# Eight copying transfers issued one stage earlier, and one weight load moved behind an exchange, in a two-layer decoder trunk

## The chip, the cores and the metric

The kernel runs on one core of one Trainium2 chip. The metric is the device time in microseconds of one execution. Before the change it is 1097.91 us as the median of three runs (1097.39 to 1098.72 us). One further execution was recorded by the hardware profiler; all rows in this document come from such recorded executions.

The engines are named as in the profile: PE is the matrix engine (PEld its weight loads), DVE the vector engine, ACT the scalar engine, POOL the GpSimd engine and SP the sync engine, which here only issues transfers.

## The reference

The input x is 512 tokens of 1024 float32 numbers. It passes two layers; each has an attention mixer and a gated feed-forward part:

```python
for i in range(DEPTH):                       # DEPTH = 2
    h = rms_norm(x, pre_g);  h = mixer_i(h);  x = x + rms_norm(h, post_g)
    h = conv_ffn(rms_norm(x, ffn_pre_g[i]), w_up, conv_w, conv_b, w_down)
    x = x + rms_norm(h, ffn_post_g[i])
```

Layer 0's mixer is latent attention beside differential attention. Layer 1's mixer is dilated attention in three groups of four heads beside stick-breaking attention with four heads. In the dilated part each group has its own softmax, and the groups are merged by weights made from all three groups' largest scores and denominators. The feed-forward part multiplies by w_up (1024 x 5632), runs a causal convolution of width 3 over the tokens, gates one half with the other, and multiplies by w_down (2816 x 1024).

## The kernel before

**Tiles.** The 512 tokens are four tiles of 128, taken in the order 3, 2, 1, 0 (ORDER, the names X[3] to X[0]). Every float32 product is made of three matrix products: a value is split into a rounded high part and the remainder, and mm3 (lines 325 to 327) issues high x high, high x low and low x high.

**Weights.** The class Weights feeds blocks of 128 x 1024. load issues one transfer on SP's queue (line 62) into a staging buffer wraw, of which there are three; split makes the parts from it, with a cast on ACT (line 84) and a subtraction on DVE (line 85), and only then is the staging buffer free. ahead says how many blocks are made beyond the one in use. W is the main list; W2, made in the second layer, holds the first two blocks of that layer's output projection and shares the staging buffers with W.

**The weight sums.** Sixteen of the 22 pairs of up-projection blocks of each layer are multiplied by a scheme with seven half-size products in place of eight, which needs sums of the quarters of w_up. The DMA engines make these sums in DRAM while the core computes: sum_steps lists eight steps (copy or accumulate) for each of six chunks of weights, and each step is one transfer of POOL's queue (line 164), of 768 KB for the first four chunks. In the list for a layer, the first step of all four chunks comes first, then the second step, and so on. Steps one and two are plain copies from the input into two different sums; step three accumulates onto the first copy. A small transfer of one number, the mark (line 173), can be put ahead: POOL's queue waits there until that number has been made, which holds back all that follow. Layer 1's first four chunks are ordered by make_sums(1, range(4), ...) in odd (line 1627): the mark, whose number comes from sv (the copy to lead, line 1626), and 32 transfers. Chunk 4 follows in odd behind a mark made of shares, and chunk 5 at the start of the second feed-forward part.

**The end of layer 0.** ffn(0) ends with the last four units of the down projection, tile by tile. The order is written out by hand for PE, DVE, ACT and POOL (the tail, from line 812 on). For each tile, part_of squares and sums on ACT and multiplies by the gain on DVE, and rstd (lines 238 to 241) makes one over the root on POOL. add_to (line 818) adds the normed result to X on DVE. Then mean_square of X (ACT, line 250, and POOL again), normed (DVE, line 822) and turned (PE transposes, line 273) make the transposed input of the next layer. r1 and r0 are the roots of tiles 1 and 0 of this norm, q1 the list of the two roots of the next layer's first norm for X[1] and X[0]. The last transposes stand between products of odd's first projection: tile_V for tiles 3, 2 and 1 calls what is in turns at its steps 4, 5 and 6. So POOL's order is r1, the root for X[1], r0, the root for X[0].

**The dilated part of layer 1.** Stick-breaking attention comes first, then the dilated groups (lines 1876 on), again in an order written by hand, SP included. Four projections cq and ck are made; score12 and softmax12 score groups 1 and 2, with the maxima and sums in st12. Those are laid out by residue of the token modulo 4, and group 0's statistics st0 by plain token tile, so the two are exchanged through DRAM: exchange(n, src) writes a small table (line 1802) and exchange_back(n, dst) reads it in the other layout (line 1805), both on SP's queue. share (lines 1786 to 1794) makes from both the weight of each group, scale0 (line 1820) and scale12 (line 1849) multiply the scores by it, and turn0 and turn12 transpose the scores on PE (lines 1830 and 1859). tile_V makes the values of groups 1 and 2 from four blocks of od_w_v12 and writes them re-ordered by transfers of SP (line 1899). In the third of the four projections stands W2.load(), which issues the load of the second block of W2. W2.next() behind the first share makes its parts (wo, from the same lines 84 and 85).

**Scheduling.** Where no order is written by hand, the framework's planner orders an engine's instructions by their dependencies and its own costs; SP's queue at the end of ffn(0) is such a case.

Of the kernel before, what the change touches and what calls it, by code (L numbers as in the profile page):

```python
# [98 lines left out]
def trunk(tc, A, out):  # L99
    nc = tc.nc  # L100
    PE, ACT, DVE, POOL = nc.tensor, nc.scalar, nc.vector, nc.gpsimd

    with ExitStack() as top:
# [28 lines left out]
        lead = cst.tile([P, 72], F32, tag="lead", name="lead")  # L132
# [13 lines left out]
        sums_of = {}  # L146

        def sum_steps(layer, chunks, mark=None, copies_first=False):

            wide = "(a q) c -> a (q c)"  # L150
            if layer not in sums_of:
                sums_of[layer] = [[dpool.tile([n * P, S], F32, tag=f"ws{layer}{j}{c}", name="ws")
                                   for c, n in enumerate(CHUNKS[layer])] for j in range(4)]
            tiles = sums_of[layer]

            def move(c, j, src, op):
                if src is None:
                    src = tiles[0][c][:]
                elif src < 0:
                    src = tiles[1][c][:]  # L160
                else:
                    at = sum(CHUNKS[layer][:c]) * P
                    src = A[f"ffn_up_q{layer}"][src, at:at + CHUNKS[layer][c] * P]
                nc.gpsimd.dma_start(tiles[j][c][:].rearrange(wide, q=4), src.rearrange(wide, q=4), accum_op=op,  # L164
                                    max_dma_last_dim=8192)

            steps = [(0, 3, ALU.bypass), (2, 2, ALU.bypass), (0, 2, ALU.add), (2, 0, ALU.add), (1, None, ALU.bypass),
                     (1, 0, ALU.add), (3, -1, ALU.bypass), (3, 1, ALU.add)]
            if copies_first:
                steps[4:] = [(1, 0, ALU.bypass), (3, 1, ALU.bypass), (1, None, ALU.add), (3, -1, ALU.add)]  # L170
            moves = [lambda c=c, step=step: move(c, *step) for step in steps for c in chunks]
            if mark is not None:
                moves.insert(0, lambda: nc.gpsimd.dma_start(tiles[0][chunks[0]][0:1, 0:1], mark))
            return moves

        def make_sums(layer, chunks, mark, left=0):
            moves = sum_steps(layer, chunks, mark)
            with tc.manual_schedule(engines={POOL.engine}):
                while len(moves) > left:
                    moves.pop(0)()  # L180
            return moves
# [20 lines left out]
                    up += [(A["ffn_w_up"][layer, f, z], 1024) for z in range(2)]  # L202
            return (up + [lambda n=n: down[layer](n) for n in range(4 * HF)])

        down, last_rstd = {}, {}
        units = []
        units += [(A["ev_w_c"][u], 832) for u in range(4)]
        units += [(A["ev_w_dqk"][0, 0], 1024), (A["ev_w_dqk"][0, 1], 1024)]
# [24 lines left out]
        def rstd(ms, more=None, r=None, eps_r=None, eps=epst):  # L233
            n = ms.shape[1]
            v = chp.tile([P, 4], F32, tag="rv", name="rv", bufs=4)
            if r is None:
                r = chp.tile([P, 4], F32, tag="rr", name="rr", bufs=4)
            POOL.tensor_tensor(v[:, :n], ms, eps[:, :n], ALU.add)  # L238
            if more is not None:
                POOL.tensor_tensor(v[:, :n], v[:, :n], more, ALU.add)  # L240
            POOL.tensor_tensor(r[:, :n], v[:, :n], mhalf[:, :n], ALU.pow)
            if eps_r is not None:
                POOL.tensor_tensor(eps_r, v[:, :n], epst[:, :n], ALU.mult)
            return r
# [147 lines left out]
        def ffn(layer, xnT, pending, final):  # L392
            with ExitStack() as es:
# [423 lines left out]
                def add_to(i, t, r):  # L817
                    DVE.scalar_tensor_tensor(X[i][:], t[:], r[:, 0:1], X[i][:], ALU.mult, ALU.add)

                def normed(i, r, t):  # L820
                    for c in (slice(0, S), slice(S, D)):
                        DVE.scalar_tensor_tensor(t[:, c], X[i][:, c], r[:, 0:1], g_next[:, c], ALU.mult, ALU.mult)
# [23 lines left out]
                c1 = bank_done("c", 1, between=turn(3, t3))  # L846
                part_of(t1, m1, 1, t1[:, S:], g_post, lambda: normed(2, q2, t2q))
                r1 = rstd(m1[:, 0:1], m1[:, 1:2])
                W.ahead(W.pos + 4)
                add_to(1, t1, r1)  # L850
                q1 = []

                def last():
                    part_of(t0, m0, 0, (uu[:, 1], c1), g_post, lambda: normed(1, q1[0], t1))
                    r0 = rstd(m0[:, 1:2], m0[:, 0:1])
                    add_to(0, t0, r0)


# [682 lines left out]
        def odd(xnT, pending, order):  # L1541
            xh, xl = xnT
            with ExitStack() as es:
# [44 lines left out]
                def proj_T(*args):  # L1588
                    for _ in T_parts(*args):
                        pass  # L1590
# [33 lines left out]
                DVE.tensor_copy(tri[:], trif[:])  # L1624

                ACT.copy(lead[0:1, 1:2], sv[0:1, 0, 0:1])
                make_sums(1, range(4), lead[0:1, 1:2])


                for u in range(2):  # L1630
# [173 lines left out]
                def exchange_back(n, dst):  # L1804
                    nc.sync.dma_start(dst[:].rearrange("p a b c -> p a (b c)"), views[n][1 - n])
# [68 lines left out]
                W2 = Weights(nc, None, [(A["od_w_out"][k], 1024) for k in range(2)], 2, wpool)  # L1874
# [5 lines left out]
                with tc.manual_schedule(engines={PE.engine, DVE.engine, ACT.engine, POOL.engine, nc.sync.engine}):  # L1880
                    for n, (x, t) in enumerate((x, t) for x in range(2) for t in (cq, ck)):
                        proj_T(t[x], (-0.125, 1.0)[t is ck], False, t is cq)
                        if n % 2 == 0:
                            softmaxes = score12(n // 2)
                        softmaxes.pop(0)()
                        if n == 1:
                            wo2.append(W2.next())
                        if n == 2:
                            W2.load()
                    exchange(1, st12)  # L1890
                    depth, W.depth = W.depth, 0
                    project = proj_V()

                    def tile_V(i, tag):
                        a = project(i, tag=tag)
                        st = chp.tile([P, 512], F32, tag="s", name="vst")
                        ACT.copy(st[:], a)
                        for r in range(4):
                            nc.sync.dma_start(cv12[32 * i:32 * i + 32, r], st[r::4, :])

                    tile_V(3, "a")
                    exchange_back(1, on)
                    for i, banks in zip((3, 2, 1, 0), ("ss", "tn", "aa", "oa")):
                        score0(i, banks)
                    exchange(0, st0)
                    tile_V(2, "s")
                    exchange_back(0, by_r)
                    W.load()
                    W.load()
                    share(st0, on, 0, slice(0, 4))  # L1910
                    for i in ORDER[:2]:
                        scale0(i)
                    wo2.append(W2.next())
                    tile_V(1, "s")
                    for i in ORDER[2:]:
                        scale0(i)
                    share(st12, by_r, 1, slice(0, 4))
                    tile_V(0, "a")

                    moves = sum_steps(1, (4,), shares[1][0:1, 0, 0:1], True)  # L1920
                    halves = [glob.tile([P, 2, 4, 256], F32, tag=tag, name="pt") for tag in ("xh", "xl")]
                    turned_to += [spare[:, 0], spare[:, 1]]
                    turned_to += [sb.tile([P, 4, 256], F32, tag=tag, name="pt")[:] for tag in ("sl", "sh")]
                    turned_to += [x[:, n] for x in halves for n in range(2)]
                    fours = [(hp, rp) for hp in range(2) for rp in range(2)]
                    pts = []
                    for n, i in enumerate(ORDER):
                        pts.append(turn0(i)())
                        scale12(*fours[n])
                        for _ in range((3, 1, 1, 1)[n]):  # L1930
                            moves.pop(0)()
                    for a in fours:
                        pts.append(turn12(*a)())
                    W.ahead(W.pos + 2)
                    oT = [bank("os"[k], "oT") for k in range(2)]
                    oG = [[ap.tile([P, S], F32R, tag=f"{t}{k}", name="og") for k in range(2)] for t in ("cq", "ck")]
                    for u in range(2):
                        for value, pt in zip([value0(i) for i in ORDER] + [value12(*a) for a in fours], pts):
                            value(pt, u)
                        split(oG[0][u][:], oG[1][u][:], oT[u])  # L1940
# [50 lines left out]
        xnT = ffn(0, *xnT, False)  # L1991
        xnT = odd(*xnT)
        ffn(1, *xnT, True)


# [99 lines left out]
```

## Time and profile before

| | |
|---|---|
| median of three runs | 1097.91 us |
| profiled execution | 1096.47 us |
| its span, first to last instruction | 1094.7 us |
| mean granted clock of PE | 0.998 |
| busy: PE, DVE, ACT, POOL | 1085.6, 907.5, 647.8, 129.1 us |
| transfers on POOL's queue | 67.1 MB |
| transfers on SP's queue | 147.7 MB |

The span is what instructions cover; the profiled execution has 1.8 us around it. A row of the timeline names start, duration, engine, line, operation, and "out<-in" by the program's tile names; what stands in brackets is the time the engine stood idle before it and what released it. A row of the waits names the waiting engine and line, what it waited for, the total, how often, and the longest. A row of the windows gives a stretch, its length, the busy time of PE, PEld, DVE, ACT and POOL, the granted clock, the share of the 16 DMA engines in use and GB/s. A row of transfers names what is moved, the queue, how many, KB each, and the median time from issue to landing.

### The profile page before, as it was taken

To read this page: it belongs to the slowest core of one execution; us is meant where nothing else is said; L and a number is where in the kernel's file an instruction comes from. 1 tells how busy PE (TensorE), PEld (TensorE's weight loads), DVE (VectorE), ACT (ScalarE), POOL (GpSimd) and SP (SyncE) were. 2 spreads that over 40 slices of the span, in tenths; PEclk is the share of its full clock that TensorE was granted. 3 is DMA by queue.
4 is the path that set the end of the run, shared out by engine and by line. 5 is a ranking of instruction groups with operands and counts; after the bars stand their busy time and mean duration, and the time that the engine had idled before them with its cause. 6 is when DMAs were issued, how large, how long until landed. Compare 5 with 4: busy or idle time off the path is not lost.

```text
span 1094.7 us, 18049 instructions
## 1 busy us (share of the span) xinstructions
PE 1085.6 (99%) x6724; PEld 956.0 (87%) x6724; DVE 907.5 (83%) x1530; ACT 647.8 (59%) x1106; POOL 129.1 (12%) x245
## 2 busy tenths in 40 slices
PE   9999999999999999999999999999999999999997
PEld 8876788898999999888888877889899999988886
DVE  6887786698999999998974775568989999999896
ACT  6565675446666765647553654655656666655561
POOL 3311134220000000000022111124100000000002
PEclk9999999999999999999999999999999999999999
DMA  7797998376565564355618999878845565535452
GB/s 267 257 249 207 259 299 223 104 219 189 174 190 177 176 195 160 125 168 173 245 40 285 274 297 297 231 218 236 234 135 182 174 196 175 188 124 173 153 194 78
DMA packets 72602, 217.26 MB, mean 198 GB/s; under 512 B 10049, under 2 KB 11201, under 8 KB 64321
## 3 DMA queue, kind: packets, MB, share of 16 engines
q1 hardware_dynamic: 61872, 147.73, 40.1%
q0 software_dynamic: 9920, 67.12, 24.5%
q10 hardware_dynamic: 720, 1.25, 0.4%
q8 instruction: 53, 0.87, 0.3%
q14 instruction: 37, 0.30, 0.1%
HBM read 208.69 MB, written 73.43 MB: 258 GB/s over the span
## 4 chain that ended last, share of the span: by engine, by line
PE 97%; DVE 1%; DMA 1%; issue 0%; ACT 0%; SPq 0%; POOLq 0%; DVEq 0%; POOL 0%; ACTq 0%
PE u L327 13%; PE u L326 12%; PE u L325 12%; PE acc L325 6%; PE acc L326 6%; PE acc L327 6%; PE apt L325 3%; PE apt L326 3%; PE apt L327 3%; PE ao L325 2%; PE ao L327 2%; PE ao L326 2%; PE sps L1175 2%; PE aqk L325 1%; PE p L327 1%; PE p L326 1%
## 5 line engine op out<-in xcount | busy, mean ns | idle before, releaser
L85 DVE TENSOR_TENSOR wl<-wraw,wh 128x1024 fp32r<-128x1024 f32 x244 | 295.0, 1216 | 43.2 <-ACT wh L84 42.9
L84 ACT CAST wh<-wraw 128x1024 fp32r<-128x1024 f32 x244 | 251.9, 1046 | 94.7 <-PE u L326 22.8
L327 PE MATMUL u<-xh,wl 128*128 128x256 f32 (+1 forms) x640 | 195.0, 305 | 0.0
L325 PE MATMUL u<-xh,wh 128*128 128x256 f32 (+1 forms) x640 | 195.0, 305 | 0.0
L326 PE MATMUL u<-xl,wh 128*128 128x256 f32 (+1 forms) x640 | 194.8, 304 | 0.0
L327 PEld LDWEIGHTS u<-xh,wl 128*128 128x128 f32 x640 | 122.2, 191 | 5.5 <-DVE wl L85 0.7
L325 PEld LDWEIGHTS u<-xh,wh 128*128 128x128 f32 x640 | 122.2, 191 | 5.0
L326 PEld LDWEIGHTS u<-xl,wh 128*128 128x128 f32 x640 | 122.3, 191 | 5.0
L327 PE MATMUL u<-gh,wl 128*128 128x256 f32 x384 | 108.7, 283 | 0.0
L325 PE MATMUL u<-gh,wh 128*128 128x256 f32 x384 | 108.7, 283 | 0.0
L326 PE MATMUL u<-gl,wh 128*128 128x256 f32 x384 | 108.7, 283 | 0.0
L326 PE MATMUL acc<-wl,gh 128*128 128x512 f32 (+1 forms) x234 | 90.8, 388 | 0.0
L327 PE MATMUL acc<-wh,gl 128*128 128x512 f32 (+1 forms) x234 | 90.6, 387 | 0.0
L325 PE MATMUL acc<-wh,gh 128*128 128x512 f32 (+1 forms) x234 | 90.2, 388 | 0.0
L238 POOL TENSOR_TENSOR rv<-ms,epst 128x1 f32<-128x1 f32 x31 | 13.1, 421 | 629.9 <-ACT junk L292 291.7
L489 ACT ACTIVATE y<-u,cw 128x512 f32<-128x512 f32 x88 | 67.6, 777 | 26.3 <-PE u L327 26.2
L325 PEld LDWEIGHTS u<-gh,wh 128*128 128x128 f32 x384 | 73.7, 192 | 0.1
L326 PEld LDWEIGHTS u<-gl,wh 128*128 128x128 f32 x384 | 73.7, 192 | 0.1
L327 PEld LDWEIGHTS u<-gh,wl 128*128 128x128 f32 x384 | 73.7, 192 | 0.0
L164 POOL DMA_DIRECT2D ws<-in_ffn_up_q x72 | 52.6, 739 | 149.8 <-DMA ws<-ws 74.7
L495 DVE SCALAR_TENSOR_TENSOR y<-u,cw,y 128x510 f32<-128x510 f32 x88 | 65.5, 746 | 2.2
L493 DVE SCALAR_TENSOR_TENSOR y<-u,cw,y 128x511 f32<-128x511 f32 x88 | 65.0, 742 | 2.0 <-ACT y L489 2.0
(400 smaller groups left out, 2478.1 us busy)
## 6 DMA issues: line engine op xcount, KB each, us to landing
ws<-in_ffn_up_q POOLq DMA_DIRECT2D x48, 768.0 KB, 12.5
wraw<-ws SPq DMA_DIRECT2D x128, 256.0 KB, 2.9
wraw<-in_ffn_up_q SPq DMA_DIRECT2D x96, 256.0 KB, 3.0
wraw<-in_ffn_w_down SPq DMA_DIRECT2D x44, 512.0 KB, 3.5
ws<-ws POOLq DMA_DIRECT2D x16, 768.0 KB, 13.1
ws<-in_ffn_up_q POOLq DMA_DIRECT2D x24, 512.0 KB, 6.3
wraw<-in_ffn_w_up SPq DMA_DIRECT2D x24, 512.0 KB, 4.7
wraw<-in_od_w_dqk SPq DMA_DIRECT2D x12, 512.0 KB, 9.7
```

The lines of the kernel that those rows point to most:

```text
L84: self.nc.scalar.copy(h[:, :w], raw[:, :w])
L85: self.nc.vector.tensor_tensor(l[:, :w], raw[:, :w], h[:, :w].bitcast(F32), ALU.subtract)
L164: nc.gpsimd.dma_start(tiles[j][c][:].rearrange(wide, q=4), src.rearrange(wide, q=4), accum_op=op, max_dma_last_dim=8192)
L238: POOL.tensor_tensor(v[:, :n], ms, eps[:, :n], ALU.add)
L325: PE.matmul(o, lh, rh, start=first, stop=False, skip_group_check=more)
L326: PE.matmul(o, lh, rl, start=False, stop=False, skip_group_check=more)
L327: PE.matmul(o, ll, rh, start=False, stop=last, skip_group_check=more)
L489: ACT.activation(y[:, z], u[z], AF.Identity, bias=c[:, 3:4], scale=c[:, 2:3])
L493: DVE.scalar_tensor_tensor(y[:, z, 1:], u[z][:, :S - 1], c[:, 1:2], y[:, z, 1:], ALU.mult, ALU.add)
L495: DVE.scalar_tensor_tensor(y[:, z, 2:], u[z][:, :S - 2], c[:, 0:1], y[:, z, 2:], ALU.mult, ALU.add)
L1175: PE.matmul(ps[z], mq[h][:, i * P:(i + 1) * P], mk[h][:, :w], start=True, stop=True)
```

## The change

The list of layer 1's weight sums for chunks 0 to 3 is made at the end of ffn(0), without the mark. Five of its transfers are issued on POOL's queue directly behind r1, and three directly behind r0; these eight are the first and second step of the four chunks, all plain copies from the input. In odd, the mark now goes to one number of another sum (the one that step five writes), and the other 24 transfers follow it. W2.load() leaves the third projection and stands behind exchange_back(1, on). No arithmetic changes.

```diff
@@ ffn, tail
                 r1 = rstd(m1[:, 0:1], m1[:, 1:2])
+                later_sums.extend(sum_steps(1, range(4)))
+                for _ in range(5):
+                    later_sums.pop(0)()
                 W.ahead(W.pos + 4)
                 add_to(1, t1, r1)
...
                     r0 = rstd(m0[:, 1:2], m0[:, 0:1])
+                    for _ in range(3):
+                        later_sums.pop(0)()
                     add_to(0, t0, r0)
@@ odd, behind the first projection
-                make_sums(1, range(4), lead[0:1, 1:2])
+                with tc.manual_schedule(engines={POOL.engine}):
+                    nc.gpsimd.dma_start(sums_of[1][1][0][0:1, 0:1], lead[0:1, 1:2])
+                    for move in later_sums:
+                        move()
@@ odd, dilated part
                             wo2.append(W2.next())
-                        if n == 2:
-                            W2.load()
                     exchange(1, st12)
...
                     tile_V(3, "a")
                     exchange_back(1, on)
+                    W2.load()
                     for i, banks in zip((3, 2, 1, 0), ("ss", "tn", "aa", "oa")):
```

More of the change, by code (lines that the diff above doesn't have):

```diff
@@ L203, in ffn_units @@
             return (up + [lambda n=n: down[layer](n) for n in range(4 * HF)])
-        down, last_rstd = {}, {}
+        down, last_rstd, later_sums = {}, {}, []
         units = []
```

## The prediction

> **What bounds the kernel now.** I read the page first: the shares of the engines, the granted clock in forty slices, and the chain of work that ended last by engine.
>
> ```profile
> PE 1085.6 (99%) x6724; PEld 956.0 (87%) x6724; DVE 907.5 (83%) x1530; ACT 647.8 (59%) x1106; POOL 129.1 (12%) x245
> PEclk9999999999999999999999999999999999999999
> PE 97%; DVE 1%; DMA 1%; issue 0%; ACT 0%; SPq 0%; POOLq 0%; DVEq 0%; POOL 0%; ACTq 0%
> ```
>
> TensorE is busy for all but 9 us of the span, at full clock, and 97% of the chain is TensorE work. A busy matmul row can hide a stall, so the next view is what the weight loads of TensorE waited for, between 540 and 800 us, the stretch that holds everything this change touches. The columns are total us, times, longest.
>
> ```profile
> PEld zp L1656 <- issue: 1.2, 2, 0.8
> PEld apt L326 <- issue: 0.8, 1, 0.8
> PEld osb L1711 <- ACT wh L84: 0.7, 2, 0.4
> PEld run L1688 <- DVE z L1699: 0.6, 2, 0.4
> PEld zp L1656 <- DVE osl L231: 0.3, 1, 0.3
> PEld z L1771 <- DVE st L1753: 0.3, 1, 0.3
> PEld t L1859 <- ACT spare L1831: 0.3, 1, 0.3
> ```
>
> The five rows that name another engine add to 0.7 + 0.6 + 0.3 + 0.3 + 0.3 = 2.2 us. The rows marked "issue" name nobody, and no transfer is named at all. So 2.2 us is about what any better order of transfers could give back here, and the question becomes whether the change touches those waits or makes new ones.
>
> Where the transfers stand is shown by the windows. The last two columns are the share of the 16 DMA engines and GB/s.
>
> ```profile
> 550.00:555.00 5.00, 5.00 (x28) 4.22 (x27) 4.18 (x7) 3.03 (x7) 2.61 (x5) 1.00 0.01 3
> 555.00:560.00 5.00, 5.00 (x28) 4.21 (x27) 5.00 (x7) 2.46 (x6) 1.06 (x2) 1.00 0.41 118
> 565.00:570.00 5.00, 5.00 (x28) 4.29 (x27) 2.95 (x5) 2.77 (x6) 0.74 (x2) 1.00 0.00 0
> 586.90:593.90 7.00, 7.00 (x32) 5.80 (x31) 2.87 (x4) 1.55 (x2) 4.08 (x9) 1.00 0.92 322
> 695.00:700.00 5.00, 5.00 (x38) 4.10 (x38) 4.93 (x31) 4.99 (x20) 0.00 (x0) 1.00 1.01 205
> ```
>
> Around the last norms of layer 0 the transfers are nearly idle. From 587 us the weight sums fill them, and at 695 us they are still full. TensorE keeps its 5.00 us of 5.00 in both.
>
> **The change part by part.** First, the POOL queue. Eight copies (five and three) now stand behind the norms' root instructions. These are the POOL rows that matter, in order of time.
>
> ```profile
> 555.64 0.87 POOL L241 TENSOR_TENSOR rr<-rv,mhalf 128x1 f32<-128x1 f32 x1
> 561.02 0.19 POOL L238 TENSOR_TENSOR rv<-ms,epst 128x1 f32<-128x1 f32 x1 [4.51 <-ACT junk L250]
> 562.75 0.94 POOL L241 TENSOR_TENSOR rr<-rv,mhalf 128x1 f32<-128x1 f32 x1
> 567.75 0.19 POOL L238 TENSOR_TENSOR rv<-ms,epst 128x1 f32<-128x1 f32 x1 [4.06 <-ACT junk L250]
> 586.91 4.07 POOL L164 DMA_DIRECT2D ws<-in_ffn_up_q  x8 [3.56 <-DMA ws<-lead]
> L164 POOL DMA_DIRECT2D ws<-in_ffn_up_q x72: 498/794/1666, 36.9 to 791.3; - x72
> ```
>
> POOL is idle for 4.51 us after the root of tile 1 (r1 at 555.64) and for 4.06 us after that of tile 0 (r0 at 562.75). An issue takes 4.07 / 8 = 0.51 us in the burst, where DVE was busy 2.87 of 7.00 us, and 0.79 us at the median. Around 556 us DVE is busy all the time, so I take the median: 5 x 0.79 = 4.0 us in a gap of 4.51, and 3 x 0.79 = 2.4 us in one of 4.06. Price on the path: 0. From below it cannot be a gain, since nothing is taken from POOL there; from above, five at the longest issue of the trace, 1.67 us, are 8.3 us and overrun the gap by 3.8 us. What is queued behind them is the root for the norm of X1 (561.02), which DVE waits for, and behind DVE the transposes of tile 1 on TensorE:
>
> ```profile
> 561.87 1.41 DVE L822 SCALAR_TENSOR_TENSOR t<-X,rr,gain 128x512 f32<-128x512 f32 x2 [0.38 <-POOL rr L241]
> 568.61 1.41 DVE L822 SCALAR_TENSOR_TENSOR t<-X,rr,gain 128x512 f32<-128x512 f32 x2 [1.15 <-POOL rr L241]
> 564.92 1.03 PE L273 MATMUL tp<-ident,t 128*128 128x128 f32 x8
> 571.93 1.03 PE L273 MATMUL tp<-ident,t 128*128 128x128 f32 x8
> ```
>
> The normed tile 1 is ready at 561.87 + 1.41 = 563.28 and its transposes begin at 564.92, a cover of 1.6 us; for tile 0 it is 571.93 - 570.02 = 1.9 us. So the upper bound is 3.8 - 1.6 = 2.2 us of stall.
>
> Second, the copies' traffic: 8 x 768 KB = 6.3 MB, at the 322 GB/s of the window at 587 about 20 us, now inside 557 to about 580 us, beside the layer's own weight loads. The tightest is the last of the four units that the stick-breaking projections use.
>
> ```profile
> 581.68 1.23 DVE L85 TENSOR_TENSOR wl<-wraw,wh 128x1024 fp32r<-128x1024 f32 x1 [2.27 <-ACT wh L84]
> 598.14 0.68 DVE L1576 SCALAR_TENSOR_TENSOR sql<-apt,sq 128x512 fp32r<-128x512 f32 x1
> ```
>
> It is split by 582.9 us, and TensorE reaches it when the projection before it ends, at 598.1 us: 15 us of cover. Even a landing later by 12.0 us, the longest whole landing of a weight load shown below, would leave 3 us. Price 0.
>
> Third, what the copies leave behind. The sums' transfers run without a gap from 587 us; with eight of them done beforehand, the other 24 begin some 3 us earlier (they no longer follow the marker's landing, the 3.56 us above) and end about 20 us earlier. So the full stretch of 695 us empties.
>
> Fourth, the late load (second block of the output projection). SyncE's queue, DVE and ACT, and the landings of the transfers in the order of issue:
>
> ```profile
> 675.42 0.33 SPq L62 DMA_DIRECT2D wraw<-in_od_w_out  x1
> 682.59 0.33 SPq L62 DMA_DIRECT2D wraw<-in_od_w_v  x1
> 691.14 1.05 ACT L84 CAST wh<-wraw 128x1024 fp32r<-128x1024 f32 x1 [1.72 <-DMA wraw<-in_od_w_v]
> 697.13 0.33 SPq L1802 DMA_DIRECT2D stat<-st  x1
> 705.98 0.39 SPq L1805 DMA_DIRECT2D on<-stat  x1
> 706.46 0.52 SPq L1802 DMA_DIRECT2D stat<-st  x1
> 708.95 0.18 DVE L1786 TENSOR_TENSOR sm<-st,on 128x16 f32<-128x16 f32 x1 [7.50 <-DMA on<-stat]
> 712.82 1.21 DVE L85 TENSOR_TENSOR wo<-wraw,wo 128x1024 fp32r<-128x1024 f32 x1
> 717.55 4.29 DVE L1849 TENSOR_SCALAR s<-s,share 128x256 f32<-128x256 f32 x16
> 718.61 3.63 PEld L1859 LDWEIGHTS t<-ident,s 128*128 128x128 f32 x32 [0.28 <-ACT spare L1831]
> wraw<-in_od_w_out SPq DMA_DIRECT2D x1, 512.0 KB, 12.0
> stat<-st SPq DMA_DIRECT2D x1, 16.0 KB, 2.6
> wraw<-in_od_w_out SPq DMA_DIRECT2D x2, 512.0 KB, 4.3
> ```
>
> The last three rows are the landing of the moved load as it stands (issued 675.42), of the second exchange (706.46) and of two later loads of its kind. Today the moved load takes the staging buffer that comes free at 675.4; the last value-weight unit must wait for another until 682.59, its cast waits for it, and behind that cast stand the last softmax and the first exchange (697.13). That exchange's landing lets the way back be issued at 705.98, so 8.8 us go to 16 KB, and DVE then stands idle for 7.50 us. With the change the unit goes out at 675.42 and the exchange meets emptier DMA engines, where 2.6 us is the nearest row. I expect DVE at L1786 to start some 5 us earlier. The moved load goes out behind the way back, at about 700 us, and lands by about 705 at the 4.3 us of the emptier row; its cast is due when the first shares are out, so it delays nobody.
>
> What TensorE gets from all this is little: its wait of 0.28 us at L1859 and the 0.3 us at L1771 (which stands behind that same last softmax) go, together 0.6 us. The other 1.6 us of named waits lie in the stick-breaking stage and follow DVE and ACT there, not a transfer. DVE's 7.5 us of idleness costs nothing today but the 0.28 us.
>
> **Sum.** The profiled execution took 1096.47 us, of which 1094.7 are the span and 1.8 lie around it. 1096.47 - 0.6 = 1095.9; the median of the three runs, 1097.91, stands 1.4 us above the profiled one, so the forecast on the scale of the runs is **1097.3 us**. The three runs alone lie 1.3 us apart; a change under 0.2%, 2.2 us, I call no change.
>
> **The rivals.** *The issues are slower beside a busy DVE.* For it: DVE is busy 5.00 of 5.00 us here, and the median issue is longer than that of the burst beside a freer DVE (0.79 against 0.51 us). Against it: no issue of the trace took over 1.67 us. At that bound the stall is 2.2 us in the first gap; three more in the second meet a cover that has moved on by the same stall, and add nothing. Time 1097.3 + 2.2 = 1099.5 us. [...]
>
> *The late load is now too late* (the slower side). It now lies ahead of the second exchange on SyncE's queue and comes after the first way back. If the traffic at 700 us stays as heavy as at 675, the way back is issued at 706 and the load lands 12.0 us later, at 718. Its cast takes 1.05 us and DVE wants it at 712.82, so it decides from a landing of 712.82 - 1.05 - 706.4 = 5.4 us on; beyond that each microsecond moves L1849 and the transposes behind it, which have no cover (the 0.28 us). Price 12.0 - 5.4 = 6.6 us: 1097.9 + 6.6 = 1104.5 us. Against it: the sums must then not have ended earlier.
>
> *More is given back.* All 2.2 us of named waits go, as the stick-breaking stage also runs beside other transfers: 1097.9 - 2.2 = 1095.7 us. Against it: those rows name DVE and ACT.
>
> *It does not do what it says.* The accumulating transfers wait for each other's landing, so the 24 left end no earlier, the exchange still takes 8.8 us, and only the order of issues differs: 1097.9 us.
>
> **How the numbers follow.** Forecast 0.68, slow issues 0.09, late load 0.08, more given back 0.08, nothing 0.07. The forecast, the slow issues and nothing all lie within 2.2 us of before: 0.84. Of the forecast I move 0.03 to slower and 0.05 to faster for the spread of the runs, and half of "more given back" (which lies on the edge) counts as same: faster 0.09, same 0.80, slower 0.11. The range from 1095.5 to 1099.9 us takes in the 2.2 us either way, and leaves out the late load.
>
> **What would show it.** Five copies between 556.5 and 561 us and three after 563.7, with the root instruction behind them at 561.0, and TensorE's transposes at 564.9 and 571.9 as before; the last transfer of the first four chunks issued well before 692 us; the value-weight load at about 675, the first exchange landing in 3 us, and DVE's L1786 well before 708.95; no wait at L1859. A weight load of TensorE that waits for POOL's root at 565, for a weight split at 582 to 605, or a cast of the moved load after 712 us would make the prediction wrong.

## The result, and the profile after

| | before | after |
|---|---|---|
| median | 1097.91 us | 1103.1 us |
| lowest to highest | 1097.39 to 1098.72 | 1102.3 to 1103.82 |
| profiled execution | 1096.47 us | 1103.82 us |
| span | 1094.7 us | 1102.0 us |

The changed kernel takes 1.0047 times as long as the kernel before (95% interval 1.0034 to 1.0060): slower, by 5.2 us between the medians, and outside the range that was given. The working below is made against the two profiled executions, which lie 7.35 us apart: that of before is below its median, that of after above.

From the page of the kernel after, busy time and the chain:

```profile
PE 1087.7 (99%) x6724; PEld 958.0 (87%) x6724; DVE 907.2 (82%) x1530; ACT 647.7 (59%) x1106; POOL 128.3 (12%) x245
...
PE 93%; DMA 3%; DVE 2%; ACT 1%; issue 0%; POOLq 0%; DVEq 0%; POOL 0%; ACTq 0%
PE u L327 12%; PE u L325 12%; PE u L326 12%; PE acc L325 6%; PE acc L326 6%; PE acc L327 6%; PE ao L325 2%; PE ao L327 2%; PE ao L326 2%; DMA wraw<-in_od_w_dqk 2%; PE sps L1180 2%; PE apt L325 2%; PE apt L326 2%; PE apt L327 2%; PE aqk L325 1%; PE p L326 1%
```

The chain was 97% TensorE; now 2% of it, some 20 us, is one kind of transfer, the loads of od_w_dqk, the weights of the dilated part. (Lines behind the insertions stand 5 to 8 higher in the kernel after: L1581 is the L1576 of before, L1629 its L1624, L1696 its L1688.)

What the weight loads of TensorE waited for between 540 and 800 us, after:

```profile
PEld apt L325 <- DVE sql L1581: 4.1, 1, 4.1
PEld run L1696 <- DVE sl L1686: 1.5, 2, 0.9
...
PEld zp L1664 <- DVE skl L1581: 0.7, 1, 0.7
```

None of the three is in the same view of before, and the two waits that the prediction wanted to see go (z behind st, t behind spare) are gone. The start of each matmul of after, less the start of the same matmul of before, gives the loss by place: nothing up to 602 us (0.4 us there, behind the wait for skl), 4.5 us at 608.07 behind the wait at apt, 6.0 by 611.2, 7.56 at 627.61 behind the waits at run; then 6.8 behind z and t, and 6.7 at the last matmul. (The other 0.7 us of the span lie behind the last matmul.) All of the loss arises between 602 and 628 us, in the stick-breaking stage.

What set its end is in the chain of waits of after, in order of time (start, duration, what):

```profile
593.56 17.68 DMA wraw<-in_od_w_dqk
...
611.33 1.05 ACT wh L84
612.38 0.50 ACT sk L1580
...
624.73 2.84 DVE sl L1686 x2
...
627.61 0.33 PE run L1696
```

A load that takes 17.68 us, its cast on ACT, and behind that cast, on the same engine, sk: the last stick-breaking projection's result, which has nothing to do with the late weights. From sk the whole stage follows, to run on TensorE. In before the same cast and the same run:

```profile
601.35 1.05 ACT L84 CAST wh<-wraw 128x1024 fp32r<-128x1024 f32 x1 [3.89 <-PE apt L326]
```

```profile
614.82 2.90 DVE L1678 TENSOR_TENSOR sl<-sp,sh 128x1280 fp32r<-128x1280 f32 x2
```

There the cast waited for TensorE to give back a buffer, not for a transfer, and sl was done at 617.72, 2.33 us before TensorE came to run at 620.05. So the cast is late by 611.33 - 601.35 = 9.98, of which 2.33 are covered: 7.65 us, and 7.56 were measured. The earlier stall at 608 has the same form one load ahead. Timeline of DVE after (the brackets give the idle time before, and its releaser):

```profile
576.80 1.22 DVE L85 TENSOR_TENSOR wl<-wraw,wh 128x1024 fp32r<-128x1024 f32 x1 [0.98 <-ACT wh L84]
585.72 0.29 DVE L1629 CAST tri<-trif 128x256 fp32r<-128x256 f32 x1 [7.69 <-DMA trif<-in_sb_tri]
585.93 3.49 DVE L85 TENSOR_TENSOR wl<-wraw,wh 128x1024 fp32r<-128x1024 f32 x3
...
606.19 1.22 DVE L85 TENSOR_TENSOR wl<-wraw,wh 128x1024 fp32r<-128x1024 f32 x1 [3.77 <-ACT wh L84]
607.33 0.68 DVE L1581 SCALAR_TENSOR_TENSOR sql<-apt,sq 128x512 fp32r<-128x512 f32 x1
```

The fourth load of od_w_dqk is cast at 605.11 (before 595.91) and split at 606.19, and sql stands behind that split. Before's sql (598.14, shown in the prediction) was done at 598.82, and the matmul that needs its bank began at 603.54: 4.72 us of cover. 9.20 - 4.72 = 4.48 us; the matmul is 4.53 late. By this working the stall alone would have been absorbed in the later one.

Why the loads are late shows at 575 to 586 us. The same cast to tri in before:

```profile
577.97 0.28 DVE L1624 CAST tri<-trif 128x256 fp32r<-128x256 f32 x1
578.19 1.22 DVE L85 TENSOR_TENSOR wl<-wraw,wh 128x1024 fp32r<-128x1024 f32 x1
```

The table behind it, 128 KB on ACT's queue, is issued at 574.76 in before and at 574.73 in after. Its landing before, then after (the last column, us), and below the latter the fifth load of od_w_dqk, issued at 593.56 (before at 587.37, when it took 7.0):

```profile
trif<-in_sb_tri ACTq DMA_DIRECT2D x1, 128.0 KB, 2.6
```

```profile
trif<-in_sb_tri ACTq DMA_DIRECT2D x1, 128.0 KB, 11.0
...
wraw<-in_od_w_dqk SPq DMA_DIRECT2D x1, 512.0 KB, 17.7
```

Windows after (us; length; busy PE, PEld, DVE, ACT, POOL; clock; share of the DMA engines; GB/s):

```profile
570.00:575.00 5.00, 5.00 (x28) 4.23 (x27) 1.70 (x4) 2.46 (x5) 0.00 (x0) 1.00 1.00 321
575.00:580.00 5.00, 5.00 (x23) 4.14 (x23) 2.05 (x2) 2.22 (x3) 0.00 (x0) 1.00 1.01 323
580.00:585.00 5.00, 5.00 (x23) 4.14 (x23) 0.00 (x0) 0.58 (x1) 0.00 (x0) 1.00 0.39 151
```

**Two links.** First: the copies, and the loads and tables that queue with them, fill the DMA engines until about 582 us, and the table, issued in the copies' tail, takes 11.0 us in place of 2.6. DVE stands idle for 7.69 us in front of its cast, and three weight splits stand behind it. A split gives back a staging buffer, of which there are three, and only then can SP issue the next load: the second load of od_w_dqk goes out at 587.17 in place of 579.44, the fifth at 593.56 in place of 587.37. Second: from 587.13 on POOL issues the accumulating transfers, and beside them the fifth load takes 17.7 us.

### The profile page after: what moved, and what is told of

Read it like the earlier page. It is cut to its first block, busy times and chain, and to the rows that moved or that the text cites. A ratio compares the mean times of both kernels' runs of the same rounds, so it can differ in the third digit from the quotient of the medians.

```text
span 1102.0 us, 18049 instructions
## 1 busy us (share of the span) xinstructions
PE 1087.7 (99%) x6724; PEld 958.0 (87%) x6724; DVE 907.2 (82%) x1530; ACT 647.7 (59%) x1106; POOL 128.3 (12%) x245
## 4 chain that ended last, share of the span: by engine, by line
PE 93%; DMA 3%; DVE 2%; ACT 1%; issue 0%; POOLq 0%; DVEq 0%; POOL 0%; ACTq 0%
PE u L327 12%; PE u L325 12%; PE u L326 12%; PE acc L325 6%; PE acc L326 6%; PE acc L327 6%; PE ao L325 2%; PE ao L327 2%; PE ao L326 2%; DMA wraw<-in_od_w_dqk 2%; PE sps L1180 2%; PE apt L325 2%; PE apt L326 2%; PE apt L327 2%; PE aqk L325 1%; PE p L326 1%
## 6 DMA issues: line engine op xcount, KB each, us to landing
ws<-in_ffn_up_q POOLq DMA_DIRECT2D x48, 768.0 KB, 12.3
```

## The experiments

The theory was that the copies cause the loss, through the two links together; the rivals were that the moved load does, or one link alone. Medians and ratios are against runs of the kernel before on the same chip, where its median was 1098.0 to 1098.5 us.

### The copies alone, and the moved load alone

e1_copies_only is the kernel after with the late load back in its old place; e2_load_only is the kernel before with the late load moved.

```diff
 e1, against after:
+                        if n == 2:
+                            W2.load()
...
-                    W2.load()
 e2, against before:
-                        if n == 2:
-                            W2.load()
...
+                    W2.load()
```

> The eight early copies alone; the late weight load stays in the third projection as before. Theory A (the copies delay the small table trif, DVE waits 7.7 us at the cast to tri, and three weight splits stand behind it) and rival B (the accumulating transfers that follow the copies come too early and slow the weight loads): 1102.5 to 1104.5 us, TensorE again waits about 4 us near 608 us. Rival C (the moved load costs the time): 1097.9 us, no wait near 608.

> The moved weight load alone; the sums are ordered as before. Theories A and B: 1097.0 to 1098.0 us, at most 0.6 us under before, from the waits at the transposes of the scores and at the scores of group 0. Rival C: 1102 to 1104 us.

Measured: e1 1102.6 us, ratio 1.0042 (1.0027 to 1.0057), the loss of the change, though its stall at 606 us is 2.27 us and not the 4 expected; e2 1097.2 us, 0.9993 (0.9983 to 1.0002), which can't be told from no change. In e2 no matmul at apt waits for sql, and the matmuls run 0.5 us ahead of before from z on, a lead that is gone at 764 us. The moved load is no part of the loss.

### The first link: the cast of the table moved

e3_cast_of_tri_late is the kernel after with DVE's cast to tri put behind the first stick-breaking scores, so that no split waits for the table; the table's raw copy gets another buffer. The eight copies, the mark and the moved load stay.

```diff
-                trif = sb.tile([P, 2, P], F32, tag="z", name="trif", bufs=2)
+                trif = sb.tile([P, 2, P], F32, tag="sl", name="trif")
...
-                DVE.tensor_copy(tri[:], trif[:])
...
+                        if u == 0 and y == 0:
+                            DVE.tensor_copy(tri[:], trif[:])
```

> The changed kernel, but the cast of the small table to tri stands in the stick-breaking part (behind its first scores, about 605 us) and no longer ahead of three weight splits; the table's raw copy has another buffer. Theory A: the loads of the next projections go out at 579 to 585 us again, TensorE's wait near 608 goes, 1096.5 to 1098.5 us. Rival B: those loads still take 11 to 18 us beside the accumulating transfers, the wait stays at 3 us or more, 1101 to 1103.5 us.

Measured: 1097.62 us, ratio 0.9999 (0.9990 to 1.0008). The table still takes 9.4 us, but nobody waits for it, and the second load goes out at 579.50. The fifth goes out at 588.07, takes 16.7 us, and its cast stands at 604.90: 3.55 us late, less 2.33 of cover 1.2. Of the new waits of TensorE, this remains:

```profile
PEld run L1696 <- DVE sl L1686: 1.3, 2, 0.7
```

The time is as theory A had it, the landings (12.3 to 18.1 us for the third to sixth loads, issued 587 to 593) as rival B had them. So the second link alone costs 1.3 us here, and the first makes it a loss of 7.6.

### The second link: the accumulating transfers held

e4_sums_held is the kernel after with the mark taken from a result of the last stick-breaking projection, so that the other 24 transfers begin at 603 us.

```diff
-                ACT.copy(lead[0:1, 1:2], sv[0:1, 0, 0:1])
...
+                ACT.copy(lead[0:1, 1:2], sk[0][0:1, 1, 0:1].bitcast(F32))
```

> The changed kernel, but the 24 remaining transfers wait for a number of the last of the four stick-breaking projections (about 603 us) in place of one of the first value projection (586 us). Theory A: DVE still waits 7.7 us at the cast to tri, but the loads issued late meet empty DMA engines; most of the loss goes, yet not by A's own account, which leaves 1 us or more: 1099 to 1102 us. Rival B: all of the loss goes, 1097 to 1098.5 us.

Measured: 1096.12 us, ratio 0.9979 (0.9970 to 0.9988): faster than both kernels and below both ranges expected. DVE's timeline of e4, and the landing of its fifth load (issued 592.15):

```profile
584.77 0.29 DVE L1629 CAST tri<-trif 128x256 fp32r<-128x256 f32 x1 [7.01 <-DMA trif<-in_sb_tri]
```

```profile
wraw<-in_od_w_dqk SPq DMA_DIRECT2D x1, 512.0 KB, 3.5
```

The first link is there, DVE idle for 7.01 us and the load out 4.8 us late, but it lands in 3.5 us, at 595.6; its cast stands at 601.05 and waits for TensorE as in before. The first link alone costs nothing. e6_tri_late_sums_held takes away both.

> Both mendings at once: the cast to tri late, and the 24 transfers held until the last stick-breaking projection. If either alone gives the loads enough time: 1095.5 to 1096.8 us, no better than holding alone. If the late start still costs something after the holding: 1094.5 to 1095.5 us.

Measured: 1096.0 us, 0.9981 (0.9971 to 0.9990). By the ratios this is no different from e4, which ran on another chip.

### What kind of traffic it is: copies first

e5_copies_before_sums is the kernel after with the other eight plain copies of the sums ahead of the accumulating transfers. These copies now come from the input, and the last eight accumulating transfers take the sources they had.

```diff
-                later_sums.extend(sum_steps(1, range(4)))
+                later_sums.extend(sum_steps(1, range(4), None, True))
...
-                    for move in later_sums:
+                    for move in later_sums[8:16] + later_sums[:8] + later_sums[16:]:
```

> The changed kernel, but of the 24 remaining transfers the eight plain copies come first (steps five and eight become copies from the input, and what they accumulated before is accumulated at the end; the sums are the same) and the eight accumulating ones that came first follow them. DVE still waits at the cast to tri, so the weight loads are still issued 7.7 us late. Revised theory (the loss takes both: the late start, and accumulating transfers beside which a load takes 11 to 18 us): the loads meet copies, land in 7 to 11 us, and most of the wait near 608 us goes: 1097.5 to 1099.5 us. Rival (any transfers beside the loads do the same): 1101.5 to 1103.5 us.

Measured: 1103.69 us, ratio 1.0053 (1.0038 to 1.0068). That is close to the rival's time, but the loss lies elsewhere. Of the stalls in the stick-breaking stage 0.2 us are left: the fifth load (issued 592.02) lands in 11.5 us and its cast stands at 603.64, 2.29 us late, about what the 2.33 cover. But now the sixteen accumulating transfers go out without a copy between them, from 595.64 to 673.38. Beside them the last load of od_w_dqk and the first two of od_w_v take 23.9, 19.7 and 20.6 us (19.4, 12.8 and 12.9 in the kernel after). Staging buffers come free late, the third load of od_w_v goes out at 672.15 (before: 664.21) and lands at 692.2, and the same kind of loss appears at the values. Waits of TensorE, the cast behind that load, and a window, of e5:

```profile
PEld apv L325 <- ACT wh L84: 4.5, 2, 3.0
PEld apv L326 <- DVE wl L85: 2.0, 2, 1.1
```

```profile
692.23 1.04 ACT L84 CAST wh<-wraw 128x1024 fp32r<-128x1024 f32 x1 [3.37 <-DMA wraw<-in_od_w_v]
```

```profile
700.00:705.00 5.00, 5.00 (x21) 3.60 (x23) 3.28 (x20) 2.98 (x10) 0.00 (x0) 0.55 0.04 8
```

The sums end no later than in the kernel after (last issue 672.58 there), and there the third value load lands at 692.1 too, but TensorE comes 7 us late to the values and does not wait. The theory had the place at 608 right and missed what came next: the order of the sums only moves the place where loads meet them.

### Holding without the early copies; the moved load with the sums held

e7_all_sums_held is the kernel before with all 32 transfers held to 603 us and the late load moved. e8_held_load_in_old_place is e4 with the late load back in the third projection.

```diff
 e7, against before (and W2.load() moved as in after):
-                ACT.copy(lead[0:1, 1:2], sv[0:1, 0, 0:1])
-                make_sums(1, range(4), lead[0:1, 1:2])
...
+                ACT.copy(lead[0:1, 1:2], sk[0][0:1, 1, 0:1].bitcast(F32))
+                make_sums(1, range(4), lead[0:1, 1:2])
 e8, against e4:
+                        if n == 2:
+                            W2.load()
...
-                    W2.load()
```

> No early copies: all 32 transfers are held until the last stick-breaking projection (about 603 us), with the late weight load moved. If the early copies are what lets the sums be held: the sums end about 16 us later than before, the exchange and the moved load stand in full traffic, and TensorE waits at the transposes of the scores: 1099 to 1104 us. If the holding alone is the gain: 1095.5 to 1097 us.

> Early copies, the 24 held as in the run before, but the late weight load in its old place. If the moved load gives its 0.3 to 0.5 us (the wait at the scores of group 0): 1096.4 to 1097.2 us. If it gives nothing: 1095.7 to 1096.4 us.

Measured: e7 1112.55 us, ratio 1.0135 (1.0120 to 1.0150). The sums, still going at 707 us, run into the exchange of statistics. Waits of TensorE, then transfers issued between 690 and 725 us, of e7:

```profile
PEld t L1830 <- DVE s L1820: 11.2, 1, 11.2
```

```profile
stat<-st SPq DMA_DIRECT2D x2, 16.0 KB, 13.9
on<-stat SPq DMA_DIRECT2D x1, 16.0 KB, 19.0
```

The place is the one expected, the loss 8 us above the range. So it is the early copies that leave room to hold the rest. e8 took 1099.07 us, 1.0006 (0.9996 to 1.0015), above both ranges expected and 2.95 us more than e4 (on another chip; the ratios differ by as much). Its last value load goes out at 682.17 (e4: 675.16), and the cast waits for it:

```profile
693.63 1.04 ACT L84 CAST wh<-wraw 128x1024 fp32r<-128x1024 f32 x1 [5.99 <-DMA wraw<-in_od_w_v]
```

In before the same load goes out at 682.59 and lands in 8.5 us; here it takes 11.4. The moved load, worth nothing that can be told alone (e2), is worth 3 us with the sums held.

### Fewer early copies

e9_five_early is the kernel after without the three copies behind r0; these follow the mark.

```diff
                     r0 = rstd(m0[:, 1:2], m0[:, 0:1])
-                    for _ in range(3):
-                        later_sums.pop(0)()
```

> The changed kernel with only the five copies behind r1 early; the three behind r0 stay in odd, ahead of the accumulating transfers and behind the mark. If the loss begins with the small table being caught by the tail of the copies: five copies are 3.9 MB, 12 us from 557, so the table issued at 574.7 lands in 2.6 us again, DVE doesn't wait, the weight loads are issued at 579 to 585 us, and the time is 1096.8 to 1098.5 us. If the later traffic alone makes the loss: 1100 us or more, with a wait at 608 us.

Measured: 1096.17 us, ratio 0.9980 (0.9970 to 0.9989). DVE's timeline and the landing of the table in e9:

```profile
577.95 0.29 DVE L1627 CAST tri<-trif 128x256 fp32r<-128x256 f32 x1
```

```profile
trif<-in_sb_tri ACTq DMA_DIRECT2D x1, 128.0 KB, 2.6
```

The table lands as in before and the fifth load goes out at 587.36, as in before. It takes 12.8 us beside the sums and lands at 600.2, just ahead of its cast (601.33). With three copies fewer the burst ends before the table is fetched (the DMA engines move 0 GB/s from 573.0 to 575.1 us, and the table is issued between 574.6 and 574.9), and a loss of 0.5% becomes a gain of 0.2%, a little more than expected. The second link is eased as well: e3's fifth load, issued within 1 us of this one, took 16.7 us; here the three copies stand ahead of the accumulating transfers.

The fifth load in all of these, and what follows from its cast (late against 601.35, less 2.33):

| | issued | took | cast at | late by | less 2.33 | measured at run |
|---|---|---|---|---|---|---|
| before | 587.37 | 7.0 | 601.35 | | | |
| after | 593.56 | 17.7 | 611.33 | 9.98 | 7.65 | 7.56 |
| e1 | 592.24 | 16.9 | 609.26 | 7.91 | 5.58 | 5.49 |
| e3 | 588.07 | 16.7 | 604.90 | 3.55 | 1.22 | 1.34 |
| e5 | 592.02 | 11.5 | 603.64 | 2.29 | none | -0.14 |
| e4 | 592.15 | 3.5 | 601.05 | -0.30 | none | -0.30 |
| e9 | 587.36 | 12.8 | 601.33 | -0.02 | none | -0.02 |

The recorded executions do not start level: at 540 us, ahead of all that was changed, the matmuls of e4 already run 0.30 us and those of e5 0.35 us ahead of before, the others in the table within 0.13. So e4's -0.30 is no gain.

## Why the prediction was wrong, step by step

**POOL's issues, price 0: right.** Timeline of POOL after:

```profile
556.44 2.64 POOL L164 DMA_DIRECT2D ws<-in_ffn_up_q  x5
561.00 0.18 POOL L238 TENSOR_TENSOR rv<-ms,epst 128x1 f32<-128x1 f32 x1 [1.93 <-ACT junk L250]
...
563.64 1.59 POOL L164 DMA_DIRECT2D ws<-in_ffn_up_q  x3
567.74 0.19 POOL L238 TENSOR_TENSOR rv<-ms,epst 128x1 f32<-128x1 f32 x1 [2.51 <-ACT junk L250]
```

An issue took 0.53 us, not the 0.79 that I chose. The roots stand where they stood, and the transposes begin at 564.90 and 571.91. The rival of slow issues falls.

**The copies' traffic, "Price 0": this step failed.** The traffic was sized well (20 us, to about 580). The cover was not. I took one unit, the one split at 581.68, and asked when TensorE multiplies with it: 15 us. That unit was cast 3.8 us later and harmed nobody. But a unit also has places in two in-order queues. The units that did the harm are needed only in the dilated part; yet their casts and splits stand in ACT's and DVE's order ahead of sk and sql (after: a cast at 611.33 and sk at 612.38, a split at 606.19 and sql at 607.33). By the table, the fifth load had 601.35 - (587.37 + 7.0) = 7.0 us to its cast and 2.33 behind it: 9.3 us of cover. It lost 6.2 us by its issue and 10.7 by its landing, 16.9 together. I bounded the landing alone, by 12.0 us; it grew by less, but I set that bound against the 15 us of the wrong unit, not against 9.3. What was missing altogether is the issue: no term of the sum let a load start late because DVE waits for a small table on another queue, and the table had no row in the prediction. Of the signs of being wrong that the prediction named, the wait for a weight split came, one step removed: TensorE waited for sql, which stands behind the split at 606.19.

**"The other 24 begin some 3 us earlier and end about 20 us earlier": half right.** The last of these issues stands at 672.58, before at 692.73. But the mark was issued at 586.53 in place of 582.72: ACT's copy for it stood behind a cast that waited 6.29 us for a load in the copies' tail. And with no copies left to go first, what began at 587.13 was the second link.

**The late load: right in mechanism, nearly right in size.** SP, then ACT, after:

```profile
703.41 0.33 SPq L1810 DMA_DIRECT2D stat<-st  x1
...
707.46 0.53 SPq L1813 DMA_DIRECT2D on<-stat  x1
708.03 0.50 SPq L62 DMA_DIRECT2D wraw<-in_od_w_out  x1
```

```profile
712.38 1.04 ACT L84 CAST wo<-wraw 128x1024 fp32r<-128x1024 f32 x1
```

From the first exchange to the way back it is 4.05 us, in place of 8.85, and the 7.5 us of DVE's idleness before the shares is 0.6. At z and t 0.7 us are regained, against the 0.6 of the sum. In a kernel that runs 7 us late part of that is only the delay (e1, with the load in its old place, regains as much); e9, which is not late, gains 0.9 there. The prediction let the move and the emptier DMA engines ease the exchange together. The runs part the two: in e1, without the move, the first exchange lands in 2.6 us and DVE does not wait at the shares; in e2, with the move alone, it lands in 9.5 us and DVE is idle for 6.99. What eased it is that the sums end earlier; the move alone gives the 0.5 us of e2 at z.

**The rivals.** None described what happened. The one on the slower side has nearly the time (1104.5 us) but not the place: e1 loses as much with that load where it was. It asked when the moved load would be late; the loss came from loads that were not moved.

**Named waits as a bound.** The prediction summed the waits of before to 2.2 us, the most that could be gained. e4 and e9 are 1.2 (0.3 of it from the start) and 1.0 us ahead at their last matmul, so this held for a gain; it can say nothing of a loss. The medians of e4 and e9 lie 2.3 and 2.4 us below those of before; where the rest of that comes from the traces don't show (the recorded execution of before, 1096.47 us, is faster than every timed run of it).

## What to carry to other kernels

When a burst of transfers is put into an idle stretch, list every transfer issued until the burst has drained, the small tables first, and for each the in-order queue in which an instruction waits for it and what stands behind (here DVE, idle for 7.69 us in front of the cast of a 128 KB table, with three weight splits behind it); the cover of a load is the least over these, not the time until TensorE reads it. Count a late issue and a slow landing as separate terms, since buffers that come free late push loads into the next busy stretch (here the fifth load went out 6.2 us late and then took 17.7 us in place of 7.0). Then end the burst before the next thing that somebody waits for: here three copies of eight decided between 0.5% lost and 0.2% gained.

## What the runs showed of the hardware

**A stall of TensorE can be followed by matmuls at half the pace.** TensorE's timeline after:

```profile
608.07 0.80 PE L325 MATMUL apt<-xh,wh 128*128 128x512 f32 x1 [3.94 <-DVE sql L1581]
608.66 0.63 PE L326 MATMUL apt<-xl,wh 128*128 128x512 f32 x1
609.09 0.63 PE L327 MATMUL apt<-xh,wl 128*128 128x512 f32 x1
...
611.75 0.40 PE L325 MATMUL apt<-xh,wh 128*128 128x512 f32 x1
611.99 0.40 PE L326 MATMUL apt<-xl,wh 128*128 128x512 f32 x1
```

and windows after:

```profile
605.00:610.00 5.00, 1.93 (x5) 1.55 (x6) 2.42 (x3) 1.54 (x2) 0.96 (x2) 0.79 1.01 252
610.00:615.00 5.00, 5.00 (x21) 4.04 (x20) 2.06 (x5) 2.83 (x3) 1.23 (x3) 0.86 1.03 255
```

Behind 3.94 us of idleness the matmuls start every 0.43 us until 611.2 and every 0.23 us after that, and the granted clock is below 1 in these windows and 1.00 in those on either side. It took 1.4 us, which here cost nothing more, as run would have waited anyway. In e1 it did cost: a single stall of 2.27 us at 606 had no such tail (the matmuls behind it start every 0.23 us, at a granted clock of 1.00 in the window from 605 to 610), but three short ones at run had. Timeline of TensorE, and a window, of e1:

```profile
622.61 0.33 PE L1696 MATMUL run<-sh,tri 128*128 128x128 f32 x1 [0.53 <-ACT sh L1684]
624.13 0.33 PE L1696 MATMUL run<-sl,tri 128*128 128x128 f32 x1 [1.20 <-DVE sl L1686]
...
625.54 0.47 PE L1696 MATMUL run<-sl,tri 128*128 128x128 f32 x1 [0.51 <-DVE sl L1686]
```

```profile
627.00:630.00 3.00, 3.00 (x9) 2.42 (x9) 1.69 (x6) 1.69 (x3) 0.00 (x0) 0.50 0.98 377
```

2.24 us of stall within 3.5 us, and a granted clock of 0.66, 0.50 and 0.70 in the windows of 3 us from 624 to 633, with matmuls at apt every 0.43 us in the middle one: the lateness goes from 5.49 to 8.4 us with no further wait. This is why e1 ends as late as the kernel after, though its loads are 2 us less late. A stall of 3.94 us in the kernel after and three short ones of 2.24 us together in e1 had such a tail, a single one of 2.27 us in e1 had none; what sets it off was not taken apart.

**Landings beside another queue's transfers.** A 512 KB load of od_w_dqk took 3.3 to 5.1 us with the sums held (e4, issued 586 to 598), 8.3 to 11.5 in e5, where plain copies go first (issued 587 to 602), and 11.1 to 17.7 in the kernel after, beside accumulating transfers (issued 588 to 602). These times seem to hold the wait behind the loads ahead as well. In the kernel after, the loads issued at 588.30, 589.44 and 593.56 land at 599.4, 605.0 and 611.2, some 6 us apart; in e5 those issued at 587.25, 588.38 and 592.02 land at 595.6, 599.2 and 603.5, some 4 us apart. In before, loads that went out 5 to 10 us apart beside accumulating transfers (issued 609 to 632) took 10.1 to 11.7 us. The DMA engines are full in the windows at 570 and at 605 (shares of 1.00 and 1.01), but move 321 GB/s with copies and 252 with accumulating transfers. Why accumulating transfers hold a load back more was not taken apart.
